# Decays from running sums whose rows are spread by DMA, and query norms from VectorE's turns and sums instead of transposes

## The chip, the cores and the metric

The kernel runs on one core of one Trainium2 chip. The core has five engines, each with an instruction stream of its own: TensorE (PE in the profile; its weight loads are shown as PEld), VectorE (DVE), ScalarE (ACT), GpSimd (POOL) and SyncE (SP), which here only starts transfers. An engine works through its instructions in the order in which they were put; what it needs of another engine or of a transfer it waits for at a semaphore. The metric is the device time of one execution in microseconds, smaller being better. Times of before and after are medians of several runs.

## The reference

The model is a trunk of two layers over 256 positions of width 2048, batch 1, all in float32. Layer 0 is a gated delta-rule attention with 16 heads of width 128, layer 1 a softmax attention. Only layer 0 is touched. Cut to what matters:

```python
proj = h @ w_in                                  # q, k, v, z, and 16 + 16 columns a_in, b_in
qkv = silu(causal_depthwise_conv(proj[..., :3 * A_INNER], conv_w))
q = l2_norm(q) * A_HEAD_DIM ** -0.5              # q / sqrt(sum(q*q) + EPS), per position and head
k = l2_norm(k)
g = -exp(a_log) * softplus(a_in + dt_bias)       # one number per position and head, negative
gc = cumsum(g)                                   # along the positions
decay = exp(where(lower triangle, gc[i] - gc[j], -inf))
lower = strictly lower part of (k_beta @ k.T) * decay
u, w = solve (I + lower) against v_beta and k_beta * exp(gc)
o = ... products of q, k, v_new with decay ...
out = (rms_norm(o, out_norm_w) * silu(z)) @ w_out
```

Two quantities concern us. One is the table of decays, exp(gc[i] - gc[j]) for every pair of positions i >= j and every head. The other is the sum of squares of each query row, one number per position and head.

## The kernel before

Everything is held transposed: features on the 128 partitions, the 256 positions along the free axis, so that a head (128 features) is one tile of 128 x 256. The weights are streamed once, in 320 chunks of 512 KB. For each chunk SyncE starts the load into `wt` (line 208, four buffers), ScalarE casts it to `whi` (line 209) and VectorE subtracts to get the remainder `wlo` (line 210); both have three buffers. TensorE then multiplies `whi` with both halves of the input and `wlo` with the larger half (`features`, `features2`, `tokens`; the matmuls are recorded at line 259). A chunk's load is emitted three chunks ahead of its use (`LOOK`).

Between the chunks the kernel does its background work. It is written as generators that stand in two lists, the lanes `bgq` and `bg2`. Every chunk emits a number of steps (`tick`, `step`), and a step takes one lane, by turns, and runs its first generator up to its next `yield`; if that lane is empty it takes the other. The instructions of a step are placed behind the matmul, the cast and the remainder that were emitted last (`behind`). The final order on each engine is made from this by the framework's scheduler when the program is built.

In layer 0 the order is: four groups of queries (four heads each; the first with 16 steps, then three pairs of blocks with 32 steps each), four groups of keys (16 steps per pair), three of the four groups of gates, four groups of values, the last of the gates, and then the output projection. The background of the first part is:

- `x_stats` (lane `bgq`): the scale of each position of the input.
- `decays` (lane `bg2`, put there after the first group of queries): 32 columns of the projection for all positions, from them g and beta on VectorE in many small instructions (lines 455 to 479), then the decay table `dec`. Positions are cut into two halves of 128, so that a head has three squares: first half with first, first with second, second with second. For each group of four heads VectorE multiplies a triangle of ones by g (lines 486 ff., split into a large and a small part), TensorE multiplies that by a triangle or by ones (line 501; six matmuls of 128 x 512 a group), which gives gc[i] - gc[j] in PSUM, ScalarE takes the exponentials (lines 506 to 510), and VectorE sets the upper triangle to zero (line 516).
- `q_conv`, `q_rest` (lane `bgq`): convolution, SiLU, and the norms of a group of queries. For the norms TensorE transposes each tile of 128 x 128 (line 552), and ScalarE squares it with a running sum along the free axis (line 558) into `ssq`.
- `k_small` (lane `bgq`), one per group of keys: convolution, products of keys with keys and queries on TensorE (line 601), times the decays on VectorE (line 605). This is the first use of `dec`. `ssq` is used later: GpSimd forms `epq` of it (line 761), which `v_back` reads.

`dl` is one tile of 48 KB per partition, with two parts for each head: part 1 holds the decays (`dec`), part 0 is filled by `k_small` with the products. The slot `tt` (16 KB) holds, one after the other, the operands of `decays` and the split keys and queries of `k_small(0)` (line 583). `work` has two buffers of the tag `cv`, in which a group of queries stands between its convolution and the end of its use. GpSimd has little to do in this part: it builds constants at the start (lines 90 to 104) and the small powers for the norms.

Of the kernel before, what the change touches and what calls it, by code (L numbers as in the profile page):

```python
# [7 lines left out]
F32 = mybir.dt.float32  # L8
F32R = mybir.dt.float32r
# [5 lines left out]
P = 128  # L15
# [24 lines left out]
def tile_hybrid_trunk(  # L40
# [29 lines left out]
    def slot(tag, kb, dt=F32):  # L70

        return big.tile([P, kb * 256], dt, name=tag, tag=tag)
# [12 lines left out]
    for _ in range(NWARM):  # L85
# [8 lines left out]
    pool.memset(lt_f, 1.0)  # L94
    pool.affine_select(out=lt_f, in_=lt_f, compare_op=ALU.is_ge, fill=0.0, base=0,
                       pattern=[[1, P]], channel_multiplier=-1)
    gt_f = abm[:, 1024 + P:1024 + 2 * P]
    pool.memset(gt_f, 1.0)
    pool.affine_select(out=gt_f, in_=gt_f, compare_op=ALU.is_gt, fill=0.0, base=0,
                       pattern=[[-1, P]], channel_multiplier=1)  # L100
    ones_f = const.tile([P, P], F32, name="ones_f")
    pool.memset(ones_f, 1.0)
    nhalf = const.tile([P, 16], F32, name="nhalf")
    pool.memset(nhalf, -0.5)
    gt_r = const.tile([P, P], F32R, name="gt_r")
    ones_r = const.tile([P, P], F32R, name="ones_r")

    def rsqrt(dst, src, scale, bias):

# [298 lines left out]
    def ht(name, dt=F32):  # L408
        return const.tile([P, H, 2], dt, name=name)

    beta, g_r, gl_r = ht("beta"), ht("g_r", F32R), ht("gl_r", F32R)

    dl = slot("dl", 48).rearrange("p (h k c) -> p h k c", h=H, k=2)
    dec = dl[:, :, 1, :]
# [3 lines left out]
        return dl[:, 4 * k:4 * k + 4, 0, :].rearrange("p h (b d) -> p h b d", d=P)[:, :, 0::2, :]  # L418

    def decays():  # L420
        act.copy(out=gt_r, in_=gt_f)
        act.copy(out=ones_r, in_=ones_f)
# [36 lines left out]
        act.activation(out=nea, in_=sm[:, C_ALOG:C_ALOG + H], func=AF.Exp)  # L459
        act.activation(out=e, in_=ay, func=AF.Exp, scale=-1.0)  # L460
        act.activation(out=eb, in_=ab[:, 16:32, :], func=AF.Exp, scale=-1.0)
        yield 1
        dve.tensor_scalar(out=z, in0=e, scalar1=2.0, scalar2=None, op0=ALU.add)
        dve.reciprocal(out=z, in_=z)
        dve.tensor_tensor(out=z, in0=z, in1=e, op=ALU.mult)
        dve.tensor_tensor(out=w2, in0=z, in1=z, op=ALU.mult)
        dve.tensor_scalar(out=q, in0=w2, scalar1=1.0 / 17.0, scalar2=None, op0=ALU.mult)
        for n in (15, 13, 11, 9, 7, 5, 3):
            dve.scalar_tensor_tensor(out=q, in0=q, scalar=1.0 / n, in1=w2, op0=ALU.add, op1=ALU.mult)
        dve.scalar_tensor_tensor(out=q, in0=q, scalar=1.0, in1=z, op0=ALU.add, op1=ALU.mult)  # L470
        dve.tensor_scalar(out=y, in0=y, scalar1=0.0, scalar2=None, op0=ALU.max)
        dve.scalar_tensor_tensor(out=q, in0=q, scalar=2.0, in1=y, op0=ALU.mult, op1=ALU.add)
        dve.scalar_tensor_tensor(out=q, in0=q, scalar=-1.0, in1=nea.unsqueeze(2).broadcast_to([P, H, 2]),
                                 op0=ALU.mult, op1=ALU.mult)
        dve.tensor_copy(out=g_r, in_=q)
        dve.tensor_tensor(out=gl_r, in0=q, in1=g_r.bitcast(F32), op=ALU.subtract)
        yield 1
        dve.tensor_scalar(out=eb, in0=eb, scalar1=1.0, scalar2=None, op0=ALU.add)
        dve.reciprocal(out=beta, in_=eb)

        rbuf = slot("tt", 16, F32R).rearrange("p (b k c) -> p b k c", b=2, k=4)

        def rhs(gi):
            for half in range(2):
                for part, src in ((0, g_r), (1, gl_r)):
                    dve.tensor_tensor(
                        out=rbuf[:, gi % 2, 2 * half + part, :].rearrange("p (h c) -> p h c", h=4),
                        in0=lt_f.unsqueeze(1).broadcast_to([P, 4, P]),
                        in1=src[:, 4 * gi:4 * gi + 4, half].bitcast(F32).unsqueeze(2).broadcast_to([P, 4, P]),
                        op=ALU.mult)  # L490

        rhs(0)
        yield 1
        rhs(1)
        yield 1
        for gi in range(4):
            hs = slice(4 * gi, 4 * gi + 4)
            ps3 = [ps_small() for _ in range(3)]
            for dst, lhs, half in ((ps3[0], gt_r, 0), (ps3[1], ones_r, 1), (ps3[2], gt_r, 1)):
                for part in range(2):  # L500
                    pe.matmul(dst, lhsT=lhs, rhs=rbuf[:, gi % 2, 2 * half + part, :],  # L501
                              start=(part == 0), stop=(part == 1))
            v0 = ps3[0].rearrange("p (h c) -> p h c", h=4)
            tail = tiny.tile([P, 4], F32, name="tail", tag="tail")
            dve.tensor_copy(out=tail, in_=v0[:, :, P - 1])
            act.activation(out=dec[:, hs, 0:128], in_=v0, func=AF.Exp)
            act.activation(out=dec[:, hs, 256:384], in_=ps3[2].rearrange("p (h c) -> p h c", h=4), func=AF.Exp)
            for i in range(4):
                act.activation(out=dec[:, 4 * gi + i, 128:256], in_=ps3[1][:, i * P:(i + 1) * P], func=AF.Exp,
                               bias=tail[:, i:i + 1])  # L510
            yield 1
            if gi < 2:
                rhs(gi + 2)
            yield 1
            for c in (0, 256):
                dve.tensor_tensor(out=dec[:, hs, c:c + 128], in0=dec[:, hs, c:c + 128],
                                  in1=lt_f.unsqueeze(1).broadcast_to([P, 4, P]), op=ALU.mult)
            yield 1

    def conv(src, i0):  # L520

# [10 lines left out]


    ssq = ht("ssq")
    qmem = {}

    def q_conv(gi, ps):
# [4 lines left out]
    def q_rest(gi):  # L542
        if gi == 0:
            qmem["q"] = slot("g", 32)[:, :H * T].rearrange("p (h t) -> p h t", h=H)
        q = qmem["q"][:, 4 * gi:4 * gi + 4, :]
        act.activation(out=q, in_=qmem[gi], func=AF.Silu)
        yield 1
        for p in range(2):
            ps = ps_small()
            for i in range(2):  # L550
                for t in range(2):
                    pe.transpose(ps[:, i * T + t * P:i * T + (t + 1) * P],
                                 q[:, 2 * p + i, t * P:(t + 1) * P], ident)
            yield 1
            for i in range(2):
                for t in range(2):
                    junk = work.tile([P, P], F32, name="sj", tag="gt")
                    act.activation(out=junk, in_=ps[:, i * T + t * P:i * T + (t + 1) * P], func=AF.Square,
                                   accum_out=ssq[:, 4 * gi + 2 * p + i, t:t + 1])
            yield 1  # L560

    imem = {}
# [686 lines left out]
```

## Time and profile before

| | |
|---|---|
| median of three runs | 1008.61 us (1008.36 to 1009.39) |
| profiled execution | 1010.83 us |
| span of its profile, first to last instruction | 1009.1 us |
| TensorE clock granted, mean | 0.997 |
| bytes read from HBM | 174.46 MB |
| bytes written to HBM | 2.10 MB |

The median comes from executions without the profiler; the profile is of one further execution, which is why its own time stands beside its span. The profile gives each engine's busy time, the chain of work that ended last (followed back from the last instruction), groups of instructions by line of the program, with their count, busy time, mean duration and the idle time of the engine ahead of them, and the transfers. Names such as `wlo<-wt,whi` tell the tile that is written and those that are read. In a row of the order of time stand the start, the duration and the engine; "x16" means that so many like instructions were merged.

### The profile page before, as it was taken

How to read it: one execution, taken by the hardware profiler on the slowest of the kernel's cores; microseconds unless marked ns; L12 is line 12 of the kernel's file. 1: busy time of each engine (PE TensorE's matmuls, PEld its weight loads, DVE VectorE, ACT ScalarE, POOL GpSimd, SP SyncE). 2: the span in 40 equal slices, each digit the busy share in tenths (PEclk: the TensorE clock that was granted, in tenths of full speed). 3: DMA queues.
4: the chain of work that ended last, by engine and by line, in shares of the span. 5: the costliest groups of instructions: out<-in, count | busy, mean ns of one | idle time of the engine just before them, and what ended most of it. 6: DMA issues, size and time to landing. Idle time of an engine off the chain costs nothing.

```text
span 1009.1 us, 15660 instructions
## 1 busy us (share of the span) xinstructions
PE 1001.4 (99%) x6090; PEld 878.8 (87%) x6090; DVE 690.0 (68%) x1121; ACT 526.6 (52%) x784; POOL 62.4 (6%) x83
## 2 busy tenths in 40 slices
PE   8999999999999999999999999999999999999998
PEld 7988888888888899899988888888888888889987
DVE  5789979997998767755867555444456666666554
ACT  6557865565446555534645444444445555555432
POOL 1000001022000000001000000000011010101000
PEclk8999999999999999999999999999999999999999
DMA  8665565555665454535765776666665565554472
GB/s 285 169 169 167 158 185 145 160 160 167 197 186 163 131 148 145 167 127 180 237 188 183 224 219 204 193 191 194 199 186 169 148 178 155 167 157 157 158 230 92
DMA packets 134186, 177.57 MB, mean 176 GB/s; under 512 B 7904, under 2 KB 90208, under 8 KB 134112
## 3 DMA queue, kind: packets, MB, share of 16 engines
q1 hardware_dynamic: 132672, 172.12, 57.5%
q0 software_dynamic: 1152, 4.19, 1.2%
q8 instruction: 47, 0.77, 0.3%
q10 hardware_dynamic: 288, 0.26, 0.1%
q14 instruction: 27, 0.22, 0.1%
HBM read 174.46 MB, written 2.10 MB: 175 GB/s over the span
## 4 chain that ended last, share of the span: by engine, by line
PE 98%; DMA 1%; DVE 0%; ACT 0%; issue 0%; SPq 0%
PE psp L259 87%; PE pss L601 2%; PE pss L259 1%; PE pss L1068 1%; DMA wt<-in_a_w_in_dram 1%; PE pss L1087 1%; PE pss L1123 1%; PE pss L833 1%; PE pss L501 1%; PE pss L1113 1%; PE pss L857 0%; PE pss L856 0%; PE pss L840 0%; PE pss L858 0%; PE pss L1086 0%; PE pss L1124 0%
## 5 line engine op out<-in xcount | busy, mean ns | idle before, releaser
L210 DVE TENSOR_TENSOR wlo<-wt,whi 128x1024 fp32r<-128x1024 f32 (+1 forms) x322 | 391.2, 1218 | 244.9 <-ACT whi L209 241.0
L209 ACT CAST whi<-wt 128x1024 fp32r<-128x1024 f32 (+1 forms) x322 | 336.7, 1046 | 381.3 <-PE psp L259 331.8
L259 PE MATMUL psp<-whi,xb 128*128 128x512 f32 x1024 | 318.9, 391 | 0.0
L259 PE MATMUL psp<-xb,whi 128*128 128x512 f32 (+1 forms) x1088 | 261.4, 382 | 2.2 <-ACT whi L209 1.9
L259 PEld LDWEIGHTS psp<-xb,whi 128*128 128x128 f32 x1088 | 197.0, 191 | 36.4 <-ACT whi L209 2.5
L259 PEld LDWEIGHTS psp<-whi,xb 128*128 128x128 f32 x1024 | 191.7, 188 | 39.1
L259 PE MATMUL psp<-wlo,xb 128*128 128x512 f32 x512 | 200.8, 392 | 0.0
L259 PE MATMUL psp<-xb,wlo 128*128 128x256 f32 x1024 | 149.0, 285 | 0.7 <-DVE wlo L210 0.7
L259 PE MATMUL psp<-g,whi 128*128 128x256 f32 (+1 forms) x736 | 149.6, 318 | 0.0
L259 PEld LDWEIGHTS psp<-xb,wlo 128*128 128x128 f32 x1024 | 138.0, 192 | 6.6 <-DVE wlo L210 1.2
L259 PEld LDWEIGHTS psp<-g,whi 128*128 128x128 f32 x736 | 121.7, 191 | 8.4 <-DVE g L900 0.2
L259 PEld LDWEIGHTS psp<-wlo,xb 128*128 128x128 f32 x512 | 96.2, 188 | 19.7
L259 PE MATMUL psp<-g,wlo 128*128 128x256 f32 x480 | 101.9, 284 | 0.3 <-DVE wlo L210 0.3
L259 PEld LDWEIGHTS psp<-g,wlo 128*128 128x128 f32 x480 | 77.8, 191 | 1.7 <-DVE wlo L210 0.5
L529 DVE SCALAR_TENSOR_TENSOR cv<-raw,sm,cv 128x255 f32<-128x255 f32 (+2 forms) x144 | 63.8, 477 | 3.4 <-ACT cv L527 3.2
L527 ACT ACTIVATE cv<-raw,sm 128x256 f32<-128x256 f32 x48 | 22.5, 509 | 20.6 <-DVE raw L345 20.6
L1051 POOL TENSOR_SCALAR ssn<-ssn,uh 128x4 f32<-128x4 f32 x16 | 8.3, 530 | 266.8 <-DVE ssn L1049 266.8
L330 DVE TENSOR_TENSOR ev<-psp,ev 128x512 f32<-128x512 f32 x33 | 22.6, 684 | 0.1
L329 ACT COPY ev<-psp 128x512 f32<-128x512 f32 x33 | 19.1, 579 | 0.0
L1099 ACT ACTIVATE raw<-raw,mx 128x128 f32<-128x128 f32 (+1 forms) x32 | 14.2, 446 | 7.4 <-DVE mx L1097 7.4
L605 DVE TENSOR_TENSOR dl<-pss,dl 128x512 f32<-128x512 f32 (+1 forms) x32 | 16.3, 551 | 2.7 <-PE pss L601 2.7
L1058 DVE TENSOR_TENSOR cv<-psp,rn 128x512 f32<-128x512 f32 x16 | 10.2, 683 | 8.9 <-POOL rn L1053 8.9
(233 smaller groups left out, 742.4 us busy)
## 6 DMA issues: line engine op xcount, KB each, us to landing
wt<-in_b_w_in_dram SPq DMA_DIRECT2D x128, 512.0 KB, 3.7
wt<-in_a_w_in_dram SPq DMA_DIRECT2D x127, 512.0 KB, 4.0
wt<-in_a_w_out_dram SPq DMA_DIRECT2D x32, 512.0 KB, 3.8
wt<-in_b_w_out_dram SPq DMA_DIRECT2D x32, 512.0 KB, 3.9
dl<-in_xT_dram POOLq DMA_DIRECT2D x4, 512.0 KB, 5.8
dl<-in_relb_dram POOLq DMA_DIRECT2D x4, 512.0 KB, 4.9
g<-in_xT_dram SPq DMA_DIRECT2D x7, 256.0 KB, 5.2
out_dram<-cv SPq DMA_DIRECT2D x2, 512.0 KB, 3.5
```

The source lines that it names most:

```text
L209: cast = act.copy(out=hi[:, js, cs], in_=wt[:, js, cs])
L210: rest = dve.tensor_tensor(out=lo[:, js, cs], in0=wt[:, js, cs], in1=hi[:, js, cs].bitcast(F32), op=ALU.subtract)
L259: state["mm"] = pe.matmul(*args, **kw).ins
L329: act.copy(out=ev, in_=ps[:, :, 1, :])
L330: dve.tensor_tensor(out=ev, in0=ps[:, :, 0, :], in1=ev, op=ALU.add)
L501: pe.matmul(dst, lhsT=lhs, rhs=rbuf[:, gi % 2, 2 * half + part, :], start=(part == 0), stop=(part == 1))
L527: act.activation(out=cv[:, i, :], in_=raw[:, i, :], func=AF.Copy, scale=conv_w(i0 + i, 3))
L529: dve.scalar_tensor_tensor(out=cv[:, i, s:], in0=raw[:, i, :T - s], scalar=conv_w(i0 + i, 3 - s), in1=cv[:, i, s:], op0=ALU.mult, op1=ALU.add)
L601: pe.matmul(dst, lhsT=kq[:, a, i, c:c + P], rhs=rhs, start=(n == 0), stop=(n == 2))
L605: dve.tensor_tensor(out=dl[:, h, :, c], in0=src.rearrange("p (k c) -> p k c", k=2), in1=dec[:, h, c].unsqueeze(1).broadcast_to([P, 2, n]), ...
L1058: dve.tensor_tensor(out=n[:, t, :].rearrange("p (h d) -> p h d", d=P), in0=ps[:, t, :].rearrange("p (h d) -> p h d", d=P), in1=rn[:, t, :] ...
L1099: act.activation(out=s[:, a:b], in_=s[:, a:b], func=AF.Exp, bias=mx[:, t:t + 1], accum_out=sums[:, t:t + 1])
```

## The change

Two things are replaced, and nothing else in the kernel is edited.

**The decays.** Instead of the differences gc[i] - gc[j] from TensorE, the kernel forms the running sums gc alone: one small matmul gives them with head and half on 32 partitions and the 128 positions along the free axis, another with the positions on partitions. VectorE copies the first to SBUF (`grow`) and the second, negated, to `ngc`. GpSimd's queue writes `grow` to a DRAM tile (`line`, 16 KB) and reads it back four times, each time eight rows to all 128 partitions, into `gb` in the slot `tt`. After nine steps without work, for each group of four heads, GpSimd copies the two diagonal squares into `dec` with a very negative number in the place of the masked part, and adds up a column `across`; ScalarE then takes exponentials of 128 x 128, three per head, with `ngc` or `across` as the bias. The triangle `gt_f`, its casts `gt_r`, `ones_r`, the split of g and the multiplications by the triangle are gone.

**The norms of the queries.** Instead of 32 transposes on TensorE and 32 squares with sums, ScalarE squares a whole group at once, in place, VectorE turns it in blocks of 32 x 32 (into the part of `dl` that the keys fill later), sums along the free axis into `parts`, and after the last group four small matmuls with a matrix `fold` (made on GpSimd at the start of this part) add up the four blocks of each head, and VectorE copies the result to `ssq`.

The diff, without the removed constants and the declarations that only give room:

```diff
-        dve.tensor_copy(out=g_r, in_=q)
-        dve.tensor_tensor(out=gl_r, in0=q, in1=g_r.bitcast(F32), op=ALU.subtract)
-        yield 1
+        gf = q.rearrange("p h t -> p (h t)")
         dve.tensor_scalar(out=eb, in0=eb, scalar1=1.0, scalar2=None, op0=ALU.add)
         dve.reciprocal(out=beta, in_=eb)
...
-        def rhs(gi):
-            for half in range(2):
-                for part, src in ((0, g_r), (1, gl_r)):
-                    dve.tensor_tensor(
...
-        rhs(0)
-        yield 1
-        rhs(1)
-        yield 1
+        yield 1
+        ps = ps_small()
+        pe.matmul(ps[0:32, 0:P], lhsT=gf, rhs=lt_f, start=True, stop=True)
+        pe.matmul(ps[:, P:P + 32], lhsT=lt_f, rhs=gf, start=True, stop=True)
+        grow = abm[0:32, 1280:1280 + P]
+        dve.tensor_copy(out=grow, in_=ps[0:32, 0:P])
+        ngc = const.tile([P, H, 2], F32, name="ngc")
+        dve.tensor_scalar(out=ngc, in0=ps[:, P:P + 32].rearrange("p (h t) -> p h t", t=2), scalar1=-1.0, scalar2=None,
+                          op0=ALU.mult)
+        line = rows.tile([32, P], F32, name="line")
+        nc.gpsimd.dma_start(out=line, in_=grow)
+        gb = slot("tt", 16).rearrange("p (j c) -> p j c", c=P)
+        for gi in range(4):
+            js = slice(8 * gi, 8 * gi + 8)
+            nc.gpsimd.dma_start(out=gb[:, js, :], in_=line[js, :].unsqueeze(0).broadcast_to([P, 8, P]))
+        for _ in range(9):
+            yield 1
+        gb = gb.rearrange("p (h t) c -> p h t c", t=2)
+        across = const.tile([P, H], F32, name="across")
         for gi in range(4):
             hs = slice(4 * gi, 4 * gi + 4)
-            ps3 = [ps_small() for _ in range(3)]
...
+            for t in range(2):
+                pool.affine_select(out=dec[:, hs, 2 * P * t:2 * P * t + P], in_=gb[:, hs, t, :], compare_op=ALU.is_ge,
+                                   fill=NEG, base=0, pattern=[[0, 4], [1, P]], channel_multiplier=-1)
+            pool.tensor_tensor(out=across[:, hs], in0=gb[:, hs, 0, P - 1], in1=ngc[:, hs, 0], op=ALU.add)
+            yield 1
+            for h in range(4 * gi, 4 * gi + 4):
+                for c, src, b in ((0, dec[:, h, 0:P], ngc[:, h, 0:1]), (P, gb[:, h, 1, :], across[:, h:h + 1]),
+                                  (2 * P, dec[:, h, 2 * P:3 * P], ngc[:, h, 1:2])):
+                    act.activation(out=dec[:, h, c:c + P], in_=src, func=AF.Exp, bias=b)
+                yield 1
...
+    parts = const.tile([P, P], F32, name="parts")
+    fold = const.tile([P, 32], F32, name="fold")
+    pool.tensor_copy(out=fold, in_=ident[:, 0:32])
+    for b in range(1, 4):
+        pool.tensor_tensor(out=fold, in0=fold, in1=ident[:, 32 * b:32 * b + 32], op=ALU.add)
...
         act.activation(out=q, in_=qmem[gi], func=AF.Silu)
         yield 1
+        sq = qmem[gi]
+        act.activation(out=sq, in_=q, func=AF.Square)
+        turn = dl[:, 4 * gi:4 * gi + 4, 0, 0:T]
+        part = parts[:, 32 * gi:32 * gi + 32]
+        yield 1
         for p in range(2):
+            hs = slice(2 * p, 2 * p + 2)
+            dve.transpose(out=turn[:, hs], in_=sq[:, hs])
+            yield 1
+        dve.reduce_sum(out=part.rearrange("p (h b) -> p h b", h=4), in_=turn.rearrange("p h (b d) -> p h b d", d=32),
+                       axis=AX.X)
+        yield 1
+        if gi == 3:
             ps = ps_small()
-            for i in range(2):
-                for t in range(2):
-                    pe.transpose(ps[:, i * T + t * P:i * T + (t + 1) * P],
-                                 q[:, 2 * p + i, t * P:(t + 1) * P], ident)
-            yield 1
-            for i in range(2):
-                for t in range(2):
-                    junk = work.tile([P, P], F32, name="sj", tag="gt")
-                    act.activation(out=junk, in_=ps[:, i * T + t * P:i * T + (t + 1) * P], func=AF.Square,
-                                   accum_out=ssq[:, 4 * gi + 2 * p + i, t:t + 1])
+            for c in range(4):
+                pe.matmul(ps[32 * c:32 * c + 32, 0:32], lhsT=fold, rhs=parts[:, c:128:4], start=True, stop=True,
+                          tile_position=(0, 32 * c))
+            dve.tensor_copy(out=ssq, in_=ps[:, 0:32].rearrange("p (h t) -> p h t", t=2))
             yield 1
```

More of the change, by code (lines that the diff above doesn't have):

```diff
@@ L96, in tile_hybrid_trunk @@
                        pattern=[[1, P]], channel_multiplier=-1)
[L97 to L100, printed above, removed]
     ones_f = const.tile([P, P], F32, name="ones_f")
@@ L104, in tile_hybrid_trunk @@
     pool.memset(nhalf, -0.5)
-    gt_r = const.tile([P, P], F32R, name="gt_r")
-    ones_r = const.tile([P, P], F32R, name="ones_r")
     def rsqrt(dst, src, scale, bias):
@@ L409, in ht @@
         return const.tile([P, H, 2], dt, name=name)
-    beta, g_r, gl_r = ht("beta"), ht("g_r", F32R), ht("gl_r", F32R)
+    beta = ht("beta")
+    rows = ctx.enter_context(tc.tile_pool(name="rows", bufs=1, space=bass.MemoryType.DRAM))
     dl = slot("dl", 48).rearrange("p (h k c) -> p h k c", h=H, k=2)
@@ L420, in decays @@
     def decays():
-        act.copy(out=gt_r, in_=gt_f)
-        act.copy(out=ones_r, in_=ones_f)
         abr = slot("tt", 16, F32R)[:, :KT * 64 + 64]
@@ L474, in decays @@
                                  op0=ALU.mult, op1=ALU.mult)
-        dve.tensor_copy(out=g_r, in_=q)
-        dve.tensor_tensor(out=gl_r, in0=q, in1=g_r.bitcast(F32), op=ALU.subtract)
-        yield 1
+        gf = q.rearrange("p h t -> p (h t)")
         dve.tensor_scalar(out=eb, in0=eb, scalar1=1.0, scalar2=None, op0=ALU.add)
         dve.reciprocal(out=beta, in_=eb)
-        rbuf = slot("tt", 16, F32R).rearrange("p (b k c) -> p b k c", b=2, k=4)
-        def rhs(gi):
-            for half in range(2):
-                for part, src in ((0, g_r), (1, gl_r)):
[L486 to L490, printed above, removed]
@@ L496, in decays @@
         for gi in range(4):
             hs = slice(4 * gi, 4 * gi + 4)
-            ps3 = [ps_small() for _ in range(3)]
[L499 to L510, printed above, removed]
-            yield 1
-            if gi < 2:
-                rhs(gi + 2)
@@ L514, in decays @@
-            yield 1
-            for c in (0, 256):
-                dve.tensor_tensor(out=dec[:, hs, c:c + 128], in0=dec[:, hs, c:c + 128],
-                                  in1=lt_f.unsqueeze(1).broadcast_to([P, 4, P]), op=ALU.mult)
-            yield 1
+            for t in range(2):
+                pool.affine_select(out=dec[:, hs, 2 * P * t:2 * P * t + P], in_=gb[:, hs, t, :], compare_op=ALU.is_ge,
+                                   fill=NEG, base=0, pattern=[[0, 4], [1, P]], channel_multiplier=-1)
@@ L547, in q_rest @@
         yield 1
-        for p in range(2):
-            ps = ps_small()
-            for i in range(2):
-                for t in range(2):
-                    pe.transpose(ps[:, i * T + t * P:i * T + (t + 1) * P],
-                                 q[:, 2 * p + i, t * P:(t + 1) * P], ident)
-            yield 1
-            for i in range(2):
-                for t in range(2):
-                    junk = work.tile([P, P], F32, name="sj", tag="gt")
-                    act.activation(out=junk, in_=ps[:, i * T + t * P:i * T + (t + 1) * P], func=AF.Square,
-                                   accum_out=ssq[:, 4 * gi + 2 * p + i, t:t + 1])
+        sq = qmem[gi]
[3 more added lines that the diff above has]
+        yield 1
+        for p in range(2):
+            hs = slice(2 * p, 2 * p + 2)
[5 more added lines that the diff above has]
+        if gi == 3:
+            ps = ps_small()
+            for c in range(4):
+                pe.matmul(ps[32 * c:32 * c + 32, 0:32], lhsT=fold, rhs=parts[:, c:128:4], start=True, stop=True,
+                          tile_position=(0, 32 * c))
+            dve.tensor_copy(out=ssq, in_=ps[:, 0:32].rearrange("p (h t) -> p h t", t=2))
             yield 1
```

## The prediction, made before the changed kernel was run

> **What bounds the kernel now.** Read the busy shares first, then the chain that ended last, by engine.
>
> ```profile
> PE 1001.4 (99%) x6090; PEld 878.8 (87%) x6090; DVE 690.0 (68%) x1121; ACT 526.6 (52%) x784; POOL 62.4 (6%) x83
> ...
> PE 98%; DMA 1%; DVE 0%; ACT 0%; issue 0%; SPq 0%
> ```
>
> TensorE is busy for 1001.4 of 1009.1 us and carries 98% of the chain. It has 7.7 us of gaps in all. So an instruction that leaves TensorE shortens the run by its issue slot, as long as nothing else then makes TensorE wait. What the change touches lies between 40 and 160 us. The stretches that matter (us; busy us of PE, PEld, DVE, ACT, POOL with counts; granted clock; DMA share; GB/s):
>
> ```profile
> 3.00:12.00 9.00, 6.83 (x35) 4.46 (x33) 3.93 (x8) 6.13 (x11) 0.27 (x1) 0.93 0.96 305
> ...
> 80.00:110.00 30.00, 30.00 (x170) 26.11 (x169) 30.00 (x51) 22.56 (x49) 0.00 (x0) 1.00 0.54 149
> 110.00:134.00 24.00, 24.00 (x148) 21.43 (x147) 17.82 (x26) 19.22 (x66) 0.00 (x0) 1.00 0.64 186
> 134.00:160.00 26.00, 26.00 (x154) 23.06 (x153) 21.45 (x30) 16.23 (x28) 0.98 (x1) 1.00 0.64 178
> ```
>
> TensorE has no gap in these 80 us. But VectorE too is busy for all of 80 to 110: two engines are full there, and which one sets the pace is decided by who waits. The waits of TensorE over the whole run (total, times, longest) that name the weight splits:
>
> ```profile
> PE psp L259 <- ACT whi L209: 1.9, 1, 1.9
> ...
> PE psp L259 <- DVE wlo L210: 1.0, 3, 0.5
> ```
>
> They come to 2.9 us, and none lies in a stretch above, where PE is full. So VectorE is full with background work that it does late; it is not yet what TensorE waits for. How far ahead the splits are is read from the order of time:
>
> ```profile
> 84.06 2.35 DVE L210 TENSOR_TENSOR wlo<-wt,whi 128x1024 fp32r<-128x1024 f32 x2
> ...
> 88.21 2.06 PE L259 MATMUL psp<-xb,wlo 128*128 128x256 f32 x16
> ...
> 118.64 3.82 PE L259 MATMUL psp<-xb,whi 128*128 128x512 f32 x16
> ...
> 124.21 3.82 PE L259 MATMUL psp<-xb,whi 128*128 128x512 f32 x16
> 126.25 1.05 ACT L209 CAST whi<-wt 128x1024 fp32r<-128x1024 f32 x1 [2.54 <-PE psp L259]
> ```
>
> Two blocks of sixteen long matmuls start 5.57 us apart, and sixteen are two chunks (eight each), so a chunk takes 2.8 us. The cast at 126.25 waited for the buffer that TensorE had just left; with three buffers it serves the third chunk on, two chunks later, so it ends 5.6 - 1.05 = 4.5 us ahead of need: ScalarE's lead. Counted off in order, the two remainders of 84.06 are those that the sixteen matmuls from 88.21 use; half of 2.35 puts the first one's end near 85.3, so VectorE's lead is 2.9 us at its busiest.
>
> **The change, part by part.** *Off TensorE.* The chain gives an instruction's issue slot (the duration holds the pipeline too), the views by line the counts:
>
> ```profile
> 94.36 0.92 PE pss L501 x4
> ...
> 116.98 0.87 PE pss L552 x8
> ...
> L501 PE MATMUL pss<-tt,gt_r 128*128 128x512 f32 x16 | 5.3, 392 | 0.0
> L552 PE MATMUL pss<-ident,g 128*128 128x128 f32 x32 | 4.3, 272 | 0.0
> L501 PE MATMUL pss<-tt,ones_r 128*128 128x512 f32 x8 | 2.6, 392 | 0.0
> ...
> 44.11 0.44 PE pss L387 x4
> ```
>
> 24 decay matmuls at 0.92/4 = 0.23 us are 5.5 us, and 32 transposes at 0.87/8 = 0.109 us are 3.5: 9.0 us go. *Onto TensorE* come six small float32 matmuls, two for the running sums and four that fold the norms. L387's two such matmuls show as four instructions at 0.11, so the first new one, also 128 wide, costs 0.22. The other five are 32 wide: ten instructions, between nothing and 1.1 us; half is taken, 0.55. Net: 9.0 - 0.8 = **8.2 us** (7.7 to 8.8).
>
> *VectorE* in the groups by line:
>
> ```profile
> L516 DVE TENSOR_TENSOR dl<-dl,kT 128x512 f32<-128x512 f32 x8 | 5.3, 676 | 0.0
> L486 DVE TENSOR_TENSOR tt<-kT,gl_r 128x512 fp32r<-128x512 f32 x8 | 5.2, 680 | 0.0
> L486 DVE TENSOR_TENSOR tt<-kT,g_r 128x512 fp32r<-128x512 f32 x8 | 5.1, 680 | 0.0
> ...
> L654 DVE STREAM_TRANSPOSE g<-g 128x1024 f32<-128x1024 f32 x1 | 2.1, 2115 | 0.2 <-ACT g L570 0.2
> ...
> L866 DVE TENSOR_REDUCE so<-dl 128x8 f32<-128x1024 f32 x2 | 2.4, 1220 | 0.9 <-ACT dl L859 0.8
> ```
>
> 5.3 + 5.2 + 5.1 = 15.6 us go. Eight turns of half L654's size come, 8 x 1.06 = 8.5, and four sums of L866's size, 4.9, with three small copies set at 0.6: 14.0. That is 1.6 less. The turns are spread over four groups of queries, two of which lie after 110, so the full stretch empties most.
>
> *ScalarE* likewise:
>
> ```profile
> L558 ACT ACTIVATE sj<-pss 128x128 f32<-128x128 f32 x32 | 8.6, 292 | 0.3 <-PE pss L552 0.3
> ...
> L509 ACT ACTIVATE dl<-pss,tail 128x128 f32<-128x128 f32 x16 | 4.5, 373 | 0.0
> L546 ACT ACTIVATE g<-cv 128x1024 f32<-128x1024 f32 x4 | 4.2, 1060 | 0.5 <-DVE kT L469 0.5
> ...
> L507 ACT ACTIVATE dl<-pss 128x512 f32<-128x512 f32 x4 | 2.4, 602 | 0.3 <-PE pss L501 0.3
> L506 ACT ACTIVATE dl<-pss 128x512 f32<-128x512 f32 x4 | 2.4, 593 | 0.5 <-DVE tail L505 0.5
> ```
>
> 8.6 + 4.5 + 2.4 + 2.4 = 17.9 go; 48 exponentials at L509's 4.5/16 = 0.28 us (13.5) and four squares at L546's size (4.2) come, 17.7: even. I cost both engines at nothing: ScalarE had 30 - 22.56 + 24 - 19.22 = 12.2 us idle from 80 to 134, VectorE 24 - 17.82 + 26 - 21.45 = 10.7 from 110 to 160. With TensorE 8.2 faster and 1.6 less work VectorE keeps about 10.7 - 8.2 + 1.6 = 4.1 us. If that cover goes, its delay is TensorE's, beyond the lead.
>
> *GpSimd and DMA* get a new path: sums to DRAM (16 KB), then back to all partitions in four pieces of 512 KB; two selects and a small add for each. Nearest rows:
>
> ```profile
> L945 POOL DMA_DIRECT2D dl<-in_xT_dram x4: 751/761/1017, 472.9 to 486.2; - x4
> ...
> wt<-in_a_w_in_dram SPq DMA_DIRECT2D x127, 512.0 KB, 4.0
> ...
> dl<-in_xT_dram POOLq DMA_DIRECT2D x4, 512.0 KB, 5.8
> ...
> out_dram<-ol SPq DMA_DIRECT2D x2, 128.0 KB, 1.7
> ...
> L95 POOL TENSOR_SCALAR_AFFINE_SELECT kT<-kT 128x128 f32<-128x128 f32 x1 | 0.3, 287 | 0.0
> ```
>
> From the sums to the first exponential: issue 0.76, write 1.7 to 5.8, issue 0.76, first piece 5.8, two selects at 0.29 (L95's) to 1.15 (four times that, for four times the elements): 9.6 to 15.4 us. Behind the waiting write issue on GpSimd stand only the reads and selects of this path; GpSimd had nothing from 80 to 134. Behind a waiting exponential on ScalarE, though, stand the casts, and for them TensorE waits. The code leaves ten steps of background work between sums and selects or exponentials. A query pair has 32 steps in eight chunks, 22.3 us, so a step is 0.7 us and ten are 7 us, or 14 where the other lane takes every second one. ScalarE is thus held for 0 to 15.4 - 7 = 8.4 us; I take 3, under its lead of 4.5, so nothing. The 2 MB beside the weights: 305 GB/s were reached early, 149 are used from 80 to 110, so 156 are free and the pieces need 13.4 us; a weight tile that lands some us late has the casts' wait for a buffer in front of it. The decays take 38 steps where they took 23; with 23 of the query lane that is 61, and two pairs have 64. GpSimd's start gains four small adds and loses two instructions, with nothing waiting.
>
> **Rivals.** [...] Look at a GpSimd instruction beside a VectorE one with two SBUF operands and without, and at the reverse:
>
> ```profile
> 173.21 1.16 POOL L625 TENSOR_SCALAR ssk<-ssk 128x8 f32<-128x8 f32 x1 [36.08 <-DVE ssk L613]
> ...
> 247.35 0.24 POOL L625 TENSOR_SCALAR ssk<-ssk 128x8 f32<-128x8 f32 x1 [16.21 <-DVE ssk L613]
> ...
> 302.68 1.46 DVE L210 TENSOR_TENSOR wlo<-wt,whi 128x1024 fp32r<-128x1024 f32 x1
> ```
>
> The same L625 takes 0.24 or 1.16 us, and an L210 that takes 1.2 elsewhere took 1.46 as a GpSimd copy ran out. Each seems to wait for the other. Eight selects (2.3 to 9.2 us) and four adds (1.0 at L625's 0.24) hold VectorE for 3.3 to 10.2; against 4.1 us of room up to 6.1 fall on TensorE: 1000.4 + 0 to 6.1, say 1003.5. For it: VectorE is full and mostly on two operands. Against: the two stretches after it have gaps. [...]
>
> *ScalarE is held behind late rows: slower.* If each of the four groups' exponentials stands in front of its rows, the hold is 8.4 for the first and 3.4 (a quarter of 13.4) for each of three others, 18.6; less the lead of 4.5, 14.1 us, so 1000.4 + 14.1 = 1014.5. It turns the sign from a total hold of 4.5 + 8.2 = 12.7 us on. For it: the path is untried here and ScalarE runs in order. Against: the first hold must be near its bound, and a group's five steps (3.5 us) already cover a piece's 3.4. [...]
>
> *The change doesn't free TensorE's time*, because VectorE's backlog sets the pace of the full stretch and TensorE merely idles where the 24 matmuls were: then 5.5 come back, 1005.9, or with the 3.5 as well about 1008. Against: a lead of 2.9 us where it is smallest.
>
> **How the numbers follow.** The profiled execution took 1010.83 us, 1.7 more than its span and 2.2 more than the median of 1008.61. The sum is made against the span: 1009.1 - 8.2 = 1000.9, profiled 1002.6; for the median 1008.6 - 8.2 = **1000.4**. Its own range is 999.8 to 1002 (net 8.8 to 7.7, and a short wait). About 0.2%, 2 us, is what a measurement can tell from no change. Chances: the forecast 0.52; the shared port 0.2 (1002 to 1006.5); freed time not kept 0.15, a third of it at 1005.9 and the rest within 2 us of before; ScalarE held 0.13, of which 0.03 end within 2 us and 0.1 above. Faster 0.52 + 0.2 + 0.05 = 0.77, same 0.13, slower 0.1. The range reaches from 999.4 to 1007.2: 0.2 is left out, nearly all above.
>
> **What would show it.** Right: lines of the decay matmuls and transposes gone, PE still full from 80 to 160, the span 8 us shorter, the key products' first matmul 8 us earlier. Port: selects of over 1.2 us, L210 above 1.3 beside them, TensorE waiting for wlo. Held: an exponential with an idle time that the row DMA or a select ends, then TensorE waiting for whi. Wrong altogether: TensorE's gaps grown by as much as its busy time fell.

## The result, and the profile after

| | before | after |
|---|---|---|
| median | 1008.57 us (1008.36 to 1009.39, 4 runs) | 1016.21 us (1015.65 to 1017.29, 4 runs) |
| span of the profile | 1009.1 us | 1014.5 us |

The ratio is 1.0076, 95% interval 1.0063 to 1.0089: the change made the kernel slower, where 1000.4 us was forecast. Lines have moved: the cast is now at L203, the remainder at L204, the main matmul at L253. From the page of after, the busy shares and the chain that ended last:

```profile
PE 993.7 (98%) x6046; PEld 870.4 (86%) x6046; DVE 685.6 (68%) x1106; ACT 526.8 (52%) x746; POOL 71.6 (7%) x102
...
PE 95%; ACT 2%; DVE 1%; issue 1%; DMA 1%; SPq 0%; DVEq 0%
```

TensorE's work fell by 1001.4 - 993.7 = 7.7 us, but its gaps grew from 7.7 us to 1014.5 - 993.7 = 20.8, by 13.1. The waits of TensorE (total, times, longest) put them in one place:

```profile
PE psp L253 <- ACT whi L203: 14.2, 3, 13.0
PE psp L253 <- DVE wlo L204: 1.3, 3, 0.8
```

The stretches of the prediction, and finer ones around the wait (busy us of PE, PEld, DVE, ACT, POOL; granted clock; DMA share; GB/s):

```profile
80.00:110.00 30.00, 22.80 (x131) 19.55 (x130) 17.40 (x27) 22.67 (x57) 9.44 (x17) 0.94 0.63 203
110.00:134.00 24.00, 18.16 (x91) 15.77 (x92) 17.89 (x26) 15.93 (x24) 0.00 (x0) 0.79 0.52 146
134.00:160.00 26.00, 26.00 (x159) 22.72 (x158) 23.14 (x33) 16.18 (x20) 0.37 (x1) 1.00 0.67 183
100.00:106.00 6.00, 2.80 (x17) 2.28 (x15) 0.00 (x0) 6.00 (x22) 1.72 (x5) 1.00 0.37 128
106.00:116.00 10.00, 0.17 (x1) 0.17 (x2) 1.13 (x1) 9.97 (x24) 0.00 (x0) 0.52 0.00 1
116.00:120.00 4.00, 4.00 (x11) 3.23 (x12) 4.00 (x6) 2.50 (x4) 0.00 (x0) 0.50 0.67 190
120.00:130.00 10.00, 10.00 (x63) 9.02 (x62) 9.60 (x17) 5.55 (x8) 0.00 (x0) 0.99 0.67 187
```

From 106 to 116 only ScalarE works, without a gap; TensorE, VectorE, GpSimd and the transfers stand still. TensorE in order of time, and ScalarE:

```profile
101.69 1.11 PE L253 MATMUL psp<-xb,wlo 128*128 128x256 f32 x8
...
115.83 3.78 PE L253 MATMUL psp<-xb,whi 128*128 128x512 f32 x8 [13.03 <-ACT whi L203]
119.41 1.44 PE L253 MATMUL psp<-xb,wlo 128*128 128x256 f32 x8
```

```profile
94.55 1.05 ACT L203 CAST whi<-wt 128x1024 fp32r<-128x1024 f32 x1 [1.93 <-issue]
95.63 1.28 ACT L499 ACT_TABLE_LOAD   x1
96.92 1.28 ACT L499 ACTIVATE dl<-dl,ngc 128x128 f32<-128x128 f32 x4
98.11 0.56 ACT L323 COPY ev<-psp 128x512 f32<-128x512 f32 x1
...
111.15 0.39 ACT L499 ACTIVATE dl<-dl,ngc 128x128 f32<-128x128 f32 x1
111.55 1.28 ACT L533 ACT_TABLE_LOAD   x1
112.84 1.06 ACT L533 ACTIVATE g<-cv 128x1024 f32<-128x1024 f32 x1
113.81 2.92 ACT L203 CAST whi<-wt 128x1024 fp32r<-128x1024 f32 x3
```

All 48 exponentials stand between two casts, with one copy among them: 14.6 us from 96.92 on, with two table loads and a SiLU 19.3 us from cast to cast. TensorE had work until 101.69 + 1.11 = 102.80 and then waited 13.0 us.

The clock adds to it. It was granted in full until 106.5, half from then to 120.1, though TensorE ran again from 115.83 on. At half clock the eight matmuls from 115.83 took 3.78 us, at full clock the next eight of their kind, from 120.69 on, 2.00; the eight with `wlo` between them took 1.44, against 1.11 at 101.69: 2.1 us in all. The clock fell 3.7 us after TensorE's last matmul had ended and came back 4.3 us after the next had begun. The profile of before happens to hold a like loss (6.8 us of half clock, from 10.7 to 17.6), so that the two profiles differ by the gaps and the work alone. In before the clock fell 1.5 us into a gap of 1.95 us (9.28 to 11.22); what sets it off is not shown. Executions of before are mostly without that loss (granted clock 1.000 in eight of the nine that stand beside e1), so for the medians the sum is about 1008.6 - 7.7 + 13.1 + 2.1 = 1016.1, where 1016.2 was measured; that it comes so close is in part luck, since the two losses are only alike.

### The profile page after: what moved, and what is told of

It is laid out like the page before. It is cut to its first block, busy times and chain, and to the rows that moved or that the text cites. A ratio compares the mean times of both kernels' runs of the same rounds, so it can differ in the third digit from the quotient of the medians.

```text
span 1014.5 us, 15552 instructions
## 1 busy us (share of the span) xinstructions
PE 993.7 (98%) x6046; PEld 870.4 (86%) x6046; DVE 685.6 (68%) x1106; ACT 526.8 (52%) x746; POOL 71.6 (7%) x102
## 4 chain that ended last, share of the span: by engine, by line
PE 95%; ACT 2%; DVE 1%; issue 1%; DMA 1%; SPq 0%; DVEq 0%
PE psp L253 84%; PE pss L594 2%; ACT dl L499 1%; PE pss L253 1%; PE pss L1061 1%; PE pss L1080 1%; PE pss L1116 1%; PE pss L826 1%; DMA wt<-in_a_w_in_dram 1%; PE pss L1106 1%; ACT whi L203 0%; DVE wlo L204 0%; PE pss L850 0%; PE pss L849 0%; PE pss L833 0%
## 5 line engine op out<-in xcount | busy, mean ns | idle before, releaser
L204 DVE TENSOR_TENSOR wlo<-wt,whi 128x1024 fp32r<-128x1024 f32 (+1 forms) x322 | 391.1, 1218 | 256.3 <-ACT whi L203 252.4
L203 ACT CAST whi<-wt 128x1024 fp32r<-128x1024 f32 (+1 forms) x322 | 335.8, 1044 | 388.5 <-PE psp L253 333.1
L253 PE MATMUL psp<-whi,xb 128*128 128x512 f32 x1024 | 318.9, 391 | 0.0
L253 PE MATMUL psp<-xb,whi 128*128 128x512 f32 (+1 forms) x1088 | 260.2, 382 | 14.9 <-ACT whi L203 14.2
L253 PEld LDWEIGHTS psp<-xb,whi 128*128 128x128 f32 x1088 | 196.0, 190 | 49.9 <-ACT whi L203 15.2
L253 PEld LDWEIGHTS psp<-whi,xb 128*128 128x128 f32 x1024 | 191.7, 188 | 39.1
L253 PE MATMUL psp<-wlo,xb 128*128 128x512 f32 x512 | 200.8, 392 | 0.0
L253 PE MATMUL psp<-g,whi 128*128 128x256 f32 (+1 forms) x736 | 149.6, 318 | 0.1
L253 PE MATMUL psp<-xb,wlo 128*128 128x256 f32 x1024 | 147.5, 284 | 1.0 <-DVE wlo L204 1.0
L253 PEld LDWEIGHTS psp<-xb,wlo 128*128 128x128 f32 x1024 | 137.2, 191 | 7.0 <-DVE wlo L204 1.5
L253 PEld LDWEIGHTS psp<-g,whi 128*128 128x128 f32 x736 | 121.7, 191 | 8.4 <-DVE g L893 0.3
L253 PEld LDWEIGHTS psp<-wlo,xb 128*128 128x128 f32 x512 | 96.1, 188 | 19.8
L253 PE MATMUL psp<-g,wlo 128*128 128x256 f32 x480 | 101.9, 284 | 0.4 <-DVE wlo L204 0.4
L253 PEld LDWEIGHTS psp<-g,wlo 128*128 128x128 f32 x480 | 77.7, 191 | 1.7 <-DVE wlo L204 0.5
L862 POOL TENSOR_TENSOR ro<-so,nhalf 128x8 f32<-128x8 f32 x4 | 6.5, 1636 | 156.0 <-DVE so L860 156.0
```

The lines of the kernel that those rows point to most:

```text
L203: cast = act.copy(out=hi[:, js, cs], in_=wt[:, js, cs])
L204: rest = dve.tensor_tensor(out=lo[:, js, cs], in0=wt[:, js, cs], in1=hi[:, js, cs].bitcast(F32), op=ALU.subtract)
L253: state["mm"] = pe.matmul(*args, **kw).ins
```

## What the experiments were to decide

The rows were not late for ScalarE. GpSimd's queue and engine in after:

```profile
86.57 0.75 POOL L480 DMA_DIRECT2D line<-kT  x1 [48.45 <-DVE ngc L477]
89.25 2.13 POOL L484 DMA_DIRECT2D tt<-line  x4 [1.93 <-PE psp L253]
95.17 2.21 POOL L492 TENSOR_SCALAR_AFFINE_SELECT dl<-tt 128x512 f32<-128x512 f32 x2 [3.79 <-DMA tt<-line]
...
100.34 1.22 POOL L492 TENSOR_SCALAR_AFFINE_SELECT dl<-tt 128x512 f32<-128x512 f32 x2
```

Theory A: the sums came late (86), the nine spare steps counted from the emission were long past, so all exponentials became ready within 5 us and the scheduler's order had them in one block ahead of the casts. Theory B: the 2 MB of rows hold up the weights; the five weight loads issued from 84 to 97 took 3.9 to 9.4 us to land, median 6.9, where the page's median is 4.0.

## The experiments

Times are medians, with the ratio to before (1008.5 to 1009.2 in these comparisons) and its interval.

**One part at a time.** First the norms alone, on the kernel before.

```diff
 (on the kernel before: only q_rest, parts and fold of the change)
```

> The kernel before with the new norms of the queries alone; parts and fold lie in free columns of abm. Both theories (A: the exponentials stand as one block ahead of the casts on ScalarE; B: the 2 MB of rows make the weights late) leave the norms out of the loss: 32 transposes at 0.109 us go, four small matmuls come (at most 0.5), so 1008.6 - 3.0 = 1005.6 us, and no wait of TensorE of over 1 us between 40 and 160 us. If the turns on VectorE were the loss, it would be slower than 1008.6.

1013.79 us, 1.0051 [1.0036, 1.0066]: a miss. The part that looked harmless loses 5 us. The decays alone, with the old norms:

```diff
 (on the kernel after: q_rest of before)
```

> The changed kernel with the old norms. A and B alike: the whole loss is here, one wait of TensorE of 12 to 14 us behind the exponentials, and the norms' 3 us are missing: 1016.2 + 3.0 = 1019.2 us. If the loss came from both parts together, under 1014.

1019.55 us, 1.0110 [1.0093, 1.0127]. The time is as expected; the wait is 9.8 us and not 12 to 14, and it is now that of the transposes for a SiLU behind the exponentials:

```profile
PE pss L534 <- ACT g L528: 9.8, 1, 9.8
```

The kernel after is e2 with the new norms, and it is 3.3 us faster: there the norms do bring the 3 us that they were to bring.

**The block against the weights.**

```diff
-        for _ in range(9):
+        for _ in range(45):
             yield 1
```

> The changed kernel with 45 steps without work in front of the selects and exponentials, where it had nine; the transfers are started where they were. A: the exponentials are now written later than the casts that run beside them, so that they stand between the casts; the wait of 13 us and the half clock behind it go, 1000.4 us (to 1002). B: the weights that were 9 us in landing are so still, 5 us longer than usual, and TensorE waits 3 us or more for them at about 100 us: 1004 or more.

1011.72 us, 1.0032 [1.0020, 1.0044]. With the exponentials spread behind eleven casts the wait of 13 us is gone; but the time is far from 1000.4.

```profile
PE psp L253 <- DVE wlo L204: 5.2, 4, 3.2
```

The time and a wait of 3.2 us would also fit what was written for B. ScalarE's order of time tells the two apart: from 95.90 up to the cast that the wait hangs on (109.16) it works without a gap, 21 exponentials, three table loads and a SiLU around a single cast. That cast waited for ScalarE itself and not for its weights, though these landed about as late as in after (median 6.7 us).

```diff
-        for gi in range(4):
-            js = slice(8 * gi, 8 * gi + 8)
-            nc.gpsimd.dma_start(out=gb[:, js, :], in_=line[js, :]...)
+        nc.gpsimd.dma_start(out=gb[:, 0:8, :], in_=line[0:8, :]...)
```

One piece of four, whose rows then serve all heads, so the decays of heads 4 to 15 are those of others.

> The changed kernel that fetches one of the four pieces of rows and uses the sums of heads 0 to 3 for all heads, so 0.5 MB in place of 2; selects, exponentials and steps as they are. A: the exponentials still become ready at one time and stand as one block, TensorE waits 9 to 13 us, 1012 to 1016 us. B: with a quarter of the rows the weights land within 5 us and the wait falls under 4 us, 1001 to 1005.

1015.63 us, 1.0069 [1.0054, 1.0084]. Three quarters of the traffic are gone, the weight loads issued from 84 to 100 land within 5.5 us again (median 4.3), and the wait has stayed, so B falls for it:

```profile
PE psp L253 <- ACT whi L203: 13.4, 2, 12.6
```

**A second loss.** What e1 and e3 lost is at the end of layer 0, in code that the change does not touch. First before, then e1, same views:

```profile
140.00:420.00 280.00, 280.00 (x1937) 243.46 (x1936) 238.38 (x439) 150.80 (x193) 23.22 (x20) 1.00 0.56 160
430.00:450.00 20.00, 19.65 (x167) 19.46 (x167) 12.10 (x19) 8.24 (x11) 1.64 (x1) 1.00 0.41 133
450.00:470.00 20.00, 20.00 (x172) 20.00 (x172) 10.96 (x15) 7.56 (x9) 1.64 (x1) 1.00 0.41 133
470.00:480.00 10.00, 9.95 (x84) 9.75 (x83) 5.70 (x7) 4.60 (x6) 1.96 (x3) 1.00 0.80 261
```

```profile
140.00:420.00 280.00, 280.00 (x1931) 242.68 (x1930) 238.03 (x440) 150.47 (x194) 23.46 (x21) 1.00 0.57 162
430.00:450.00 20.00, 18.02 (x137) 17.32 (x136) 10.58 (x18) 6.08 (x8) 1.64 (x1) 0.91 0.34 112
450.00:470.00 20.00, 20.00 (x173) 20.00 (x172) 9.54 (x13) 7.92 (x10) 1.64 (x1) 1.00 0.33 109
470.00:480.00 10.00, 8.44 (x70) 7.99 (x68) 5.68 (x8) 3.99 (x5) 1.79 (x2) 1.00 0.76 226
```

In e1 TensorE is full up to 420; its 2000th main matmul starts 7.0 us ahead of before (423.1 against 430.1), its 2300th 2.0 us behind. Between 430 and 480 it has 49.6 - 46.46 = 3.1 us more of gaps; half clock comes with them. Two waits there name what is late, the gated values that the output projection reads:

```profile
PE psp L259 <- DVE g L911: 0.8, 1, 0.8
PE psp L259 <- ACT g L910: 0.7, 1, 0.7
```

Their chain goes back to the inversion, whose first step on VectorE (L665 in before) began at 255.7 us in before, 258.0 in e1 and 259.0 in e3. Theory C took VectorE for the cause: the turns and sums load it ahead of the inversion. Four kernels were to test that. e5 is after with 40 spare steps and the old norms; e8 the same with the new norms; e6 puts turns and sums on the kernel before, for nothing; e7 takes the norms from another place:

```diff
 e6, in q_rest of before:
+            dve.transpose(out=turn[:, hs], in_=q[:, hs])
+            dve.reduce_sum(out=abm[:, 2304:2320]..., in_=turn[:, hs]..., axis=AX.X)
 e7, in q_rest of e5:
+        act.activation(out=sq, in_=q, func=AF.Square)
+        pe.matmul(ps[...], lhsT=sq[:, c:c + P], rhs=ones_r, start=True, stop=True)   # 8 per group
```

> The kernel after with 40 spare steps in place of 9, and with the old norms (transposes on TensorE, squares on ScalarE); nothing is left out. Seen so far: from the last scaled row block of layer 0 to the end of the span every kernel takes the same (536.6 to 537.0 us), and from the first step of the inversion on VectorE to that block 212 to 217 us; the inversion began at 255.7 in before, 258.0 with the new norms alone and 259.0 with new norms and 45 spare steps, although TensorE was 5 and 8 us ahead there. Theory C (VectorE paces the stage before the inversion; the turns and sums of the norms, 5.3 + 4.9 us, are on it): without them the inversion begins at 249 to 252, no gap of TensorE at 430 to 480, about 1004 (1003 to 1006). Rival D (the spare steps themselves, or the decays that end late, hold the chain): inversion at 259 as with 45 steps and about 1013 to 1015, since TensorE also has its transposes back (+3.5). Both: no wait of 13 us on a cast.

1007.50 us, 0.9988 [0.9979, 0.9997]: inversion at 252.4 and no gap at 430 to 480, as C has it, but 1.5 us above its range, since ScalarE, busy for 19.99 of the 20 us from 100 to 120, still cost TensorE 2.6 us there.

> The kernel before, with the turns and sums on VectorE added beside the old norms (8 turns, 8 sums of half the size; their result is used nowhere); TensorE's work is that of before. C: about 10 us more on VectorE ahead of the inversion: it begins 3 to 8 us later than in before, TensorE gets gaps at 430 to 480, 1011 to 1016, about the time of the new norms alone (1013.8). Rival D: VectorE has room, 1008.5 as before.

1014.28 us, 1.0059 [1.0047, 1.0072]; inversion at 258.9. C is met, it seems: VectorE's work alone, with TensorE's untouched, costs 5.5 us.

> As e5, but the norms of the queries from 32 TensorE matmuls of the squares (rounded to fp32r) against two columns of ones, one square of 128x1024 for each group on ScalarE, one copy of 128x8 on VectorE: neither the turns on VectorE nor the transposes of 0.109 us. C: VectorE as light as in e5 and TensorE the same or up to 2 us lighter: 1002 to 1005. D: 1011 or more.

1009.71 us, 1.0007 [0.9998, 1.0015]: a miss. No gap at 430 to 480, but a matmul of two columns takes 3.9/32 = 0.12 us, no less than a transpose, and a wait of 1.6 us for the square is new.

> The kernel after with 40 spare steps in place of 9: e5 with the new norms, so that the two differ in the norms alone. C: VectorE has the 10.2 us of turns and sums: inversion at about 258 to 259, gaps of TensorE at 430 to 480, 1010 to 1013, so 6 to 8 us slower than e5 although TensorE has 3.5 us less to do. D: 3.5 us faster than e5.

1011.68 us, 1.0030 [1.0019, 1.0041]; inversion at 257.3, gaps at 430 to 480, 4.2 us slower than e5. C again, in a smaller size.

**Exponentials made short.** e9 lets GpSimd add the bias, so that ScalarE takes 12 exponentials of 512 columns; e10 is that with the new norms, so the whole change but for the place of the bias; e11 is e10 without turns and sums (the sums of squares are set to one, so it leaves the norms of the queries out).

```diff
+            for c, src, b in ((0, gb[:, hs, 0, :], ngc[:, hs, 0]), (P, gb[:, hs, 1, :], across[:, hs]),
+                              (2 * P, gb[:, hs, 1, :], ngc[:, hs, 1])):
+                pool.tensor_tensor(out=dec[:, hs, c:c + P], in0=src, in1=b..., op=ALU.add)   # then select in place
-            for h in range(4 * gi, 4 * gi + 4):
...
+            for c in range(3):
+                act.activation(out=dec[:, hs, c * P:c * P + P], in_=dec[:, hs, c * P:c * P + P], func=AF.Exp)
+                yield 1
```

> The rows and decays of after, its 9 spare steps kept, the old norms; the bias of the exponentials is added by GpSimd (12 adds of 128x512 beside its 8 selects, which now work in place), so that ScalarE takes 12 exponentials of 128x512 in place of 48 of 128x128. Theory A (the block of ScalarE made the wait): 48 x 0.388 = 18.6 us become about 12 x 0.55 = 6.6 us, ready one after another and not all at once: no wait of 13 us, TensorE's 5.5 - 0.8 = 4.7 us are kept but for a wait of 1 us, inversion at 250 to 252, 1003 to 1006. If the wait for the rows or the weights beside them is what holds TensorE, it stays: 1015.

1009.38 us, 1.0009 [1.0000, 1.0018]. The 13 us are gone with the nine steps unchanged, so the block made them, not the rows. But ScalarE now stood idle for 5.5 us ahead of exponentials that GpSimd had not readied, with casts behind, and TensorE got 4.5 us of gaps between 90 and 130: above the range.

> e9 with the new norms, so the whole change with the bias moved to GpSimd. Theory C (VectorE paces the inversion): 10.2 us more on VectorE, inversion at 256 to 259, gaps of TensorE at 430 to 480: 1008 to 1012. Without C: 3.5 us faster than e9, 1000 to 1002.

1008.85 us, 0.9997 [0.9987, 1.0006]: in the range forecast under C, but for another reason, and here C falls. The inversion begins at 252.2, not at 256 to 259, and there is no second loss:

```profile
140.00:420.00 280.00, 280.00 (x1929) 243.17 (x1928) 237.50 (x437) 150.48 (x193) 23.16 (x20) 1.00 0.57 162
430.00:450.00 20.00, 19.65 (x167) 19.46 (x167) 12.69 (x23) 8.11 (x10) 1.64 (x1) 1.00 0.41 132
450.00:470.00 20.00, 19.94 (x171) 19.74 (x169) 11.23 (x15) 8.58 (x11) 2.31 (x2) 1.00 0.42 137
470.00:480.00 10.00, 10.00 (x83) 10.00 (x84) 7.11 (x11) 5.64 (x11) 1.74 (x3) 1.00 0.95 294
```

VectorE has the turns and sums of e8. From 140 to 420 it is busy for 238.4 us in before, 238.0 in e1 and 237.5 here: it is no fuller where the loss is.

> e10 without its 8 turns and 4 sums on VectorE (the sums of squares are set to one, so the norms of the queries are left out); TensorE's work is that of e10. C: inversion at 247 to 250, no gaps at 430 to 480, and the whole saving of the prediction's sum is there: 999 to 1002, 8 to 10 us faster than e10. Without C: the same as e10.

1005.73 us, 0.9971 [0.9961, 0.9982], 3.1 faster than e10: more than nothing, less than C asked for. What the 3.1 us are is open: the two profiled executions are only 0.4 us apart in span (1005.6 and 1005.2), and the executions of e10 spread from 1006.55 to 1010.85 with granted clocks of 1.000 to 0.994, where those of e11 have 0.998 or more.

**The order.** What sets the kernels apart is found by counting, in TensorE's order of time, the main matmuls ahead of the last of the 96 products of the keys and ahead of the inversion's first matmul:

| kernel | last key product behind | inversion's first matmul behind | TensorE busy, 430 to 480 |
|---|---|---|---|
| before, after, e2, e4, e5, e7, e9, e10, e11 | 1195 | 1480 | 49.6 to 49.7 of 50 in each |
| e6, e8 | 1210 | 1512 | 46.5, 46.4 |
| e1 | 1219 | 1520 | 46.5 |
| e3 | 1231 | 1544 | 46.1 |

Theory O: the scheduler's order, fixed when the program is built, holds these products behind more main matmuls, and so the inversion and all that follows is late. Three more readings of the traces fit it. TensorE has no gap from 140 to 420 in any of these kernels, so no product there waited for anything but its turn. The inversion's first step on VectorE begins 9.8 to 11.0 us after the last product in all of them. And from the 2000th to the 2300th main matmul e1, e3, e6 and e8 fall back against before by 9.0, 8.0, 10.3 and 7.6 us, in part with work that was put off until then, in part by the gaps; the others do not fall back at all (0.0). After belongs to the others.

e14 changes nothing but spare steps in e10, e12 moves the exponentials to where GpSimd is through, e13 is e12 with the old norms.

```diff
 e14, in e10:
-        for _ in range(9):
+        for _ in range(56):
 e12, in e10 (emitted from bg2 after the last group of queries):
+    def exps():
+        for k in range(12):
+            hs, c = slice(4 * (k // 3), 4 * (k // 3) + 4), k % 3
+            act.activation(out=dec[:, hs, c * P:c * P + P], in_=dec[:, hs, c * P:c * P + P], func=AF.Exp)
+            if k % 2 == 1:
+                yield 1
```

> e10 with 56 spare steps in place of 9: no instruction more or fewer. The later steps put the work of the keys and the inversion later in each engine's queue. Theory O (the order written at build decides the second loss, not the load of VectorE): the last product of the keys stands behind main matmul 1220 or more (1195 in e10), the inversion's first matmul behind 1540 or more (1480), gaps of TensorE at 430 to 480 of 5 us or more, 1012 to 1020. If the load decides: as e10, 1007 to 1009.

1012.55 us, 1.0030 [1.0019, 1.0042]. Not one instruction more than e10, and the last key product stands behind main matmul 1243, the inversion's first behind 1584; VectorE has 236.58 us from 140 to 420. The second loss is back, the largest of all (11.2 us from the 2000th to the 2300th main matmul), though the gaps are 4.7 us and not the 5 or more that were expected:

```profile
430.00:450.00 20.00, 17.51 (x142) 16.53 (x142) 11.71 (x22) 6.08 (x8) 1.64 (x1) 1.00 0.32 103
450.00:470.00 20.00, 20.00 (x172) 19.93 (x170) 9.27 (x13) 7.60 (x9) 1.64 (x1) 1.00 0.35 117
470.00:480.00 10.00, 7.77 (x60) 6.96 (x59) 5.75 (x8) 3.36 (x4) 1.67 (x2) 1.00 0.61 209
```

So the order is enough to make it. It is not that the decays themselves came too late: the last exponential ends at 157.7, and the first product is multiplied by them from 165.7 on. Why the scheduler takes this order in some kernels and not in others wasn't settled: VectorE's work does it in e6 and the spare steps in e14 (so D had a point, by way of the order), the turns and sums do not in e10.

> e10 with the 12 wide exponentials taken out of the decays and emitted, two to a step, after the third group of queries (from the second list, where it is otherwise empty); all other work is that of e10. In e10 the exponentials stood in ScalarE's queue ahead of GpSimd's adds being done (5 us of ScalarE's idle time ahead of them), the casts behind them, and TensorE had 4.8 us of gaps at 100 to 130. If that placing is what is left of the loss: those gaps fall under 1.5 us, no gaps at 430 to 480 (the last product of the keys again stands behind main matmul 1195 or fewer), 1001 to 1004, faster than before. If the rows, GpSimd or the weights beside them hold the casts: the gaps stay, 1006 to 1009 as e10.

1007.54 us, 0.9987 [0.9978, 0.9996]: faster than before, but 3.5 above the range's end. One gap of 4.2 us before a remainder is left at 114.6, with 6.8 us of half clock from 117.6 on. The order is that of e10 (1195 and 1480), and there is no second loss.

> e12 with the old norms. If VectorE has room for the turns and sums once the order is the same: 2 to 3.5 us slower than e12 (TensorE has its 32 transposes back). If VectorE's 10.2 us cost something in themselves: equal to e12 or faster.

1004.64 us, 0.9956 [0.9942, 0.9969], 2.9 faster than e12 though TensorE has its transposes back: here the new norms cost more than they free. That is no general price of theirs: with the order alike, they gain 3.3 us in after against e2, and in e10 against e9 the difference (0.5 faster) is within the noise. This version is faster than both kernels. Its page, and its waits, where besides the start's only three rows of 1.1 us or less in total are left:

```profile
PE 995.8 (99%) x6070; PEld 873.8 (87%) x6070; DVE 685.7 (68%) x1093; ACT 523.3 (52%) x770; POOL 92.1 (9%) x110
```

```profile
PE pss L86 <- DVE kT L83: 1.3, 1, 1.3
PE psp L253 <- ACT whi L203: 1.1, 1, 1.1
PE psp L253 <- DVE wlo L204: 1.1, 2, 0.8
PE psp L253 <- DVE ev L324: 0.2, 1, 0.2
```

## Why the prediction was wrong

*TensorE, net 8.2 us (7.7 to 8.8):* right, at the lower end; 7.7. e13 keeps the decays' part: its sum is 5.5 less the two small matmuls of the running sums, about 5, and it is 4.5 us faster than before in the median.

*The path of the rows, 9.6 to 15.4 us:* right; from the issue of the write at 86.57 to the first exponential at 96.92 it took 10.4. Weights that landed late beside the rows cost nothing that e4 could take back.

*VectorE 1.6 less, ScalarE even:* right in sum. ScalarE's busy time went from 526.6 to 526.8, VectorE's from 690.0 to 685.6. The turns were cheaper than thought, 5.3 us and not 8.5:

```profile
L542 DVE STREAM_TRANSPOSE dl<-cv 128x512 f32<-128x512 f32 x8 | 5.3, 692 | 0.0
L544 DVE TENSOR_REDUCE parts<-dl 128x32 f32<-128x1024 f32 x4 | 4.9, 1214 | 0.0
```

*"I cost both engines at nothing":* this step failed. It set 12.2 us of ScalarE's idle time, scattered over 54 us, against work that came in one block. The sums were equal; what changed was how far apart the pieces stand. Before, each group's exponentials waited for its own matmuls and so lay between casts; after, all 48 became ready together. A block of 14.6 us meets not the idle time of a stretch but the lead of the casts, 4.5 us. From the end of one cast to the start of the next it was 18.2 us with the table loads and the SiLU; less the lead that is an estimate of 13.7, and the term that was put at nothing measured 13.0, with 2.1 of half clock on top.

*"ScalarE is thus held for 0 to 8.4 us; I take 3":* mis-thought, too. It set the steps between emission and use against the time of the path. The steps were spent before the sums were there (86 us), and ScalarE was not held at all: it was busy.

*Rival "held behind late rows", 1014.5 at a chance of 0.1:* right in place and sign (casts behind exponentials on ScalarE, then TensorE) and 1.7 off in time, but wrong in its mechanism: it priced waiting, and found it unlikely; it should have priced the block, 14.6 plus the table loads less the lead, and the half clock after it.

*Rival "the shared port", 1003.5 at a chance of 0.2:* no run shows a port; what the runs show are longer instructions where GpSimd and VectorE work side by side. They cost nothing visible in after. One of the eight selects took 1.61 us beside VectorE's work, the others 0.63; the one remainder beside them took 1.25, and from 99.4 on VectorE stood still. They are in e12, where GpSimd adds as well; L204 there between 93 and 122, and in e13 from 140 to 200, where GpSimd has none of the adds and selects and is busy for 6.6 of the 60 us (minimum, median, maximum ns):

```profile
L204 DVE TENSOR_TENSOR wlo<-wt,whi x8: 1204/1648/2060, 93.8 to 120.6; 128x1024 fp32r<-128x1024 f32 x8
```

```profile
L204 DVE TENSOR_TENSOR wlo<-wt,whi x20: 1216/1223/1229, 140.7 to 199.6; 128x1024 fp32r<-128x1024 f32 x20
```

So beside the adds and selects a remainder took 1.65 us in the median, without them 1.22. e10 agrees, with 1.54 us from 93 to 122. But e13 has the longer remainders too, with no wait for one in TensorE of over 0.8 us:

```profile
L204 DVE TENSOR_TENSOR wlo<-wt,whi x10: 1212/1636/2092, 87.6 to 114.8; 128x1024 fp32r<-128x1024 f32 x10
```

So they alone do not make the gap of e12. There VectorE has the turns and sums as well, and a cast at 103.03 had waited 2.8 us for its weights; which of the three makes up the 3 us was not tried by itself.

*Rival "the freed time isn't kept":* it happens, at another place and by another cause than the one named: 300 us later, by the order (e1, e3, e6, e8, e14). In after itself it does not happen: its products stand behind 1195 and 1480 main matmuls, and TensorE is busy 49.6 of the 50 us from 430 to 480.

## What to carry over

Work that moves on an engine is priced twice where the engine keeps to the order of its queue, as ScalarE did in after (the transfers had stopped by 103.4, and the casts stood behind the exponentials until 113.81): by its sum, and by the longest piece that stands ahead of an instruction on the critical path, against that path's lead; equal sums say nothing. Spare steps count from where they are written, not from where the data arrive; if several pieces come to hang on one transfer, they come ready together and want to be placed apart, or made fewer and wider. Where a scheduler fixes the order, compare the order far behind the edit as well: a loss there (here 4 to 5 us) need not be a property of the new instructions.

## What was not expected of the hardware

The granted clock turned gaps into more: a gap of 4.2 us in e12 brought 6.8 us of half clock, 5.6 of them with matmuls, the one of 13.0 in after 13.6, but no more than 4.3 of them with matmuls. A GpSimd add of 128x512 took 1.04 us or 2.02, in e13:

```profile
103.81 2.02 POOL L494 TENSOR_TENSOR dl<-tt,across 128x512 f32<-128x512 f32 x1
...
112.53 1.04 POOL L494 TENSOR_TENSOR dl<-tt,across 128x512 f32<-128x512 f32 x1
```
